# VectorE and ScalarE in program order in two MLPs, with each Strassen bank evicted behind its last product

## The chip, the cores and the metric

The kernel runs on one core of a Trainium2 chip. The metric is the device time of one execution in microseconds; the kernel before took 2025.13 us (median of 3 runs, 2024.51 to 2026.55).

## What is computed

A decoder trunk of two layers over 256 positions of width 2048, all in float32. Each layer is a mixer (a gated MLP in the first, sliding-window attention in the second), a layer norm, an MLP and another layer norm. The change touches the two MLPs:

```python
def sq_relu_mlp(x, w_up, w_down):          # w_up: 2048 x 8192, w_down: 8192 x 2048
    return jnp.square(jax.nn.relu(x @ w_up)) @ w_down

x = layer_norm(DEEPNORM_ALPHA * x + mix, ...)
x = layer_norm(DEEPNORM_ALPHA * x + sq_relu_mlp(x, mlp_w_up[layer], mlp_w_down[layer]), ...)
```

## The kernel before, in words

**Weights.** Every weight arrives as a tile of 128 x 1024 float32 numbers. So that TensorE can multiply at its faster rate without losing float32's accuracy, each is split into two parts: ScalarE casts the high part (`w_hi`, L109) and VectorE subtracts it from the tile to get the low part (`w_lo`, L111). One such pair is an *operand*. The class `Weights` makes operands ahead of their use: there are 9 slots for them in an MLP (5, and 4 lent), and `get()` first fills all slots that are free and then hands out the next operand, so an operand is made when the one nine places before it has been used. Unsplit tiles have 4 buffers of their own, and 4 more in pairs ("wide").

**An MLP** runs in 7 chunks of its inner width. Each of the first six takes 1024 columns:

1. *Up*: 4 products (c = 0 to 3), each of 4 operands, accumulate in a PSUM tile `ps_c`. `act` then adds the two halves of the sum (ScalarE copies one, `part`; VectorE adds, `full`), takes relu and square on ScalarE, splits the result in high and low (`hT`), forms sums and differences of blocks (`sums`) and splits those too.
2. *Strassen round*: half the output columns by Strassen's scheme: 14 operands, here called s0 to s13 in the order in which they are made. Some are sums of tiles, so VectorE adds tiles (L107) before it splits. They make 7 products in 7 PSUM banks, each from two operands: s0 to s6 are the first halves, s7 to s13 the second halves of products o0 to o6. Banks are held in pairs: one PSUM tile holds o0 and o1, the next o2 and o3, then o4 and o5, the last o6 alone.
3. *Evictions*: after the whole round each bank is added to `held` or to `x` on VectorE (L472, L466; in the first chunk four of them are copied by ScalarE instead, L469).
4. *Rows*: the other output columns, two products (n = 2 and 3) of 4 operands each, called r0 to r7 here, in PSUM tiles `ps_r`; each is added to `x` (L421).

PSUM tiles come from two tags with two buffers each, `mm` and `aux`. A round uses all four. The tile of rows n = 2 takes the `mm` buffer of the round's first tile (o0 and o1), so it waits for the evictions of both.

The seventh chunk takes 2048 columns, all by rows. After the sixth, `strassen_end` combines the held products in 8 VectorE operations.

**Order.** The code is written in one sequence, and a scheduler reorders it for each engine by priority and by its own idea of when inputs are ready; each engine then runs its own list strictly in order, with semaphores between the lists. `Weights.dma` keeps the transfers in program order.

Of the kernel before, what the change touches and what calls it, by code (L numbers as in the profile page):

```python
# [11 lines left out]
F32 = mybir.dt.float32  # L12
# [41 lines left out]
class Weights:  # L54
# [4 lines left out]

    def __init__(self, tc, pool, wide, tiles, homes, operands):  # L60
        self.tc, self.nc, self.pool, self.wide = tc, tc.nc, pool, wide
        self.tiles, self.homes, self.operands = tiles, homes, operands
        self.others, self.by_pool = [], ()
        self.borrowed, self.borrowed_from = [], 0
# [29 lines left out]
    def ahead(self, n_split=None):  # L94
# [3 lines left out]
        while self.n_split < min(n_split, len(self.operands)):  # L98
# [53 lines left out]
    def get(self, ahead=None):  # L152
# [3 lines left out]
        self.load(len(self.tiles))  # L156
        hi, lo, kind = self.parts.pop(n)
# [11 lines left out]
def trunk(ctx: ExitStack, tc: tile.TileContext, t, out):  # L169
# [12 lines left out]
    def add_tiles(new):  # L182
        for w in new:
            tiles.append(w)
            homes.append("w")
            operands.append((len(tiles) - 1, None, (len(tiles) - 1,)))

    def add_strassen(new, home):
# [5 lines left out]
        operands.extend([(r, None, ()), (r, r + 1, ()), (r + 1, r + 2, (r + 1,)), (r + 2, None, ()),  # L194
                         (r, r + 2, (r + 2,)), (r + 3, None, ()), (r, r + 3, (r, r + 3))])
# [161 lines left out]
    def gather_halves(ps, bias=None, full=None):  # L357
# [8 lines left out]
        if full is None:  # L366
            full = work.tile([P, 2, S], F32, tag="full", name="full")
# [74 lines left out]
    def strassen_round(hT, groups, n, held, first, scale):  # L442

        tiles = [psum.tile([P, 2, 512], F32, tag=tag, name="ps_s")
# [14 lines left out]
        own = {3: (0, 1, ALU.subtract), 5: (0, 0, ALU.add), 6: (1, 0, ALU.add)}  # L461
        for o, bank in enumerate(banks):
            if o in own:
                tok, c, op = own[o]
                a = x[:, tok, (n + c) * 512:(n + c + 1) * 512]
                nc.vector.scalar_tensor_tensor(out=a, in0=a, scalar=scale, in1=bank,  # L466
                                               op0=ALU.mult, op1=op)
            elif first:
                nc.scalar.copy(out=held[:, HELD.index(o), :], in_=bank)  # L469
            else:  # L470
                a = held[:, HELD.index(o), :]
                nc.vector.tensor_tensor(out=a, in0=bank, in1=a, op=ALU.add)  # L472
# [4 lines left out]
    def strassen_end(n, held):  # L477
# [4 lines left out]
        for out, a, b, op in ((m6, m6, m1, ALU.subtract), (x11, x11, m1, ALU.add),  # L482
# [3 lines left out]
            nc.vector.tensor_tensor(out=out, in0=a, in1=b, op=op)  # L486

    def mlp(x, xT, extra, norm, loads, tags, end):
# [3 lines left out]
        helds = {}  # L492
        for fc, (width, rounds) in enumerate(CHUNKS):
            last = fc == len(CHUNKS) - 1

            def act(c, ps):
                if not rounds:
                    full = gather_halves(ps)
                    nc.vector.scalar_tensor_tensor(out=full, in0=full, scalar=0.0, in1=full,
                                                   op0=ALU.max, op1=ALU.mult)  # L500
                    split(hT[:, 2 * c:2 * c + 2, 0:S], hT[:, 2 * c:2 * c + 2, S:], full)
                    return

                full = gather_halves(ps)
                nc.scalar.activation(out=full, in_=full, func=AF.Relu)
                nc.scalar.activation(out=full, in_=full, func=AF.Square)
                a = full.rearrange("p b (t q) -> p (b t) q", t=NT)
                split(hT[:, c, 0, 0:4], hT[:, c, 1, 0:4], a)
# [445 lines left out]
```

## Time and profile before

| | |
|---|---|
| time, median of 3 runs | 2025.13 us |
| the profiled execution's own time | 2026.41 us |
| its span on the core | 2024.7 us |
| TensorE (PE) busy | 1949.3 us, 96% |
| VectorE (DVE) busy | 1527.6 us, 75% |
| ScalarE (ACT) busy | 1069.5 us, 53% |
| mean granted TensorE clock | 0.981 of full |

PE's busy time counts pipelined products by modelled ends, so it says when PE had work, not how fast it went. The other engines' shares are means over stages that differ; what counts is who is waited for in each stage.

### The profile page before, as it was taken

The numbers are of one execution on the slowest core, as the hardware profiler recorded it, in microseconds if no ns is written. First come the engines' busy times: TensorE is split into PE (matmuls) and PEld (weight loads), VectorE is DVE, ScalarE is ACT, GpSimd is POOL, SyncE is SP. The second block draws the span as 40 slices with busy tenths as digits, with TensorE's granted clock in tenths as the row PEclk, the third lists the DMA queues.
The fourth block names the chain that finished last, engine by engine and source line by source line (L and its number), as shares of the span: only waits on it lengthen the run. The fifth ranks groups of instructions, "written<-read, shape, count | busy, mean of one in ns | idle before, by whom it ended". The sixth has DMA issues, their size and how long they took to land.

```text
span 2024.7 us, 26597 instructions
## 1 busy us (share of the span) xinstructions
PE 1949.3 (96%) x10244; PEld 1670.2 (82%) x10244; DVE 1527.6 (75%) x1749; ACT 1069.5 (53%) x1364; POOL 103.1 (5%) x63
## 2 busy tenths in 40 slices
PE   9999999999999999999998899999999999999997
PEld 7888888878788787888897878888787878878886
DVE  5676689797878869665778997897877868796555
ACT  5445447555555645443456675465555646554431
POOL 0000010000000000000123320100000000000001
PEclk9999999999999999999998899999999999999999
DMA  8755845746556474766443336557565464747662
GB/s 327 271 180 160 286 146 172 255 160 197 176 175 216 156 221 156 240 187 194 149 148 111 97 105 229 177 176 242 175 188 183 157 203 155 252 132 249 187 187 84
DMA packets 105968, 377.57 MB, mean 186 GB/s; under 512 B 12272, under 2 KB 12912, under 8 KB 105840
## 3 DMA queue, kind: packets, MB, share of 16 engines
q1 hardware_dynamic: 105840, 375.86, 56.9%
q8 instruction: 80, 1.31, 0.3%
q14 instruction: 48, 0.39, 0.1%
HBM read 373.72 MB, written 2.10 MB: 186 GB/s over the span
## 4 chain that ended last, share of the span: by engine, by line
issue 82%; PE 8%; DVE 5%; ACT 2%; POOL 1%; DMA 0%; SPq 0%; POOLq 0%; ACTq 0%; DVEq 0%
PE ps_r L274 2%; PE ps_r L272 2%; PE ps_r L273 2%; PE ps_c L309 1%; DVE w_lo L111 1%; ACT p L763 1%; PE ps_c L318 1%; DVE x L400 0%; POOL rstd L381 0%; DVE qT L837 0%; DVE top L754 0%; POOL x L396 0%; DVE es L758 0%; POOL x L395 0%; DMA w_raw<-in_win_v 0%
## 5 line engine op out<-in xcount | busy, mean ns | idle before, releaser
L111 DVE TENSOR_TENSOR w_lo<-w_raw,w_hi 128x1024 fp32r<-128x1024 f32 (+1 forms) x643 | 784.7, 1231 | 340.2 <-ACT w_hi L109 337.6
L109 ACT CAST w_hi<-w_raw 128x1024 fp32r<-128x1024 f32 (+1 forms) x657 | 687.2, 1052 | 581.9 <-PE ps_r L274 208.8
L313 PE MATMUL ps_c<-yT,w_hi 128*128 128x512 f32 x960 | 337.6, 398 | 0.0
L313 PE MATMUL ps_c<-oT,w_hi 128*128 128x512 f32 x960 | 337.6, 398 | 0.0
L272 PE MATMUL ps_r<-w_hi,hT 128*128 128x512 f32 x640 | 255.4, 399 | 31.1 <-DVE held L472 31.1
L318 PE MATMUL ps_c<-oT,w_lo 128*128 128x256 f32 x992 | 272.5, 281 | 0.0
L318 PE MATMUL ps_c<-yT,w_lo 128*128 128x256 f32 x992 | 272.5, 281 | 0.0
L274 PE MATMUL ps_r<-w_hi,hT 128*128 128x512 f32 x640 | 253.5, 396 | 0.0
L273 PE MATMUL ps_r<-w_lo,hT 128*128 128x512 f32 x640 | 253.4, 396 | 0.0
L313 PEld LDWEIGHTS ps_c<-yT,w_hi 128*128 128x128 f32 x960 | 178.9, 188 | 42.1
L313 PEld LDWEIGHTS ps_c<-oT,w_hi 128*128 128x128 f32 x960 | 178.9, 188 | 42.0
L318 PEld LDWEIGHTS ps_c<-yT,w_lo 128*128 128x128 f32 x992 | 187.4, 189 | 2.7
L318 PEld LDWEIGHTS ps_c<-oT,w_lo 128*128 128x128 f32 x992 | 187.4, 189 | 2.7
L272 PEld LDWEIGHTS ps_r<-w_hi,hT 128*128 128x128 f32 x640 | 123.1, 192 | 60.2 <-DVE held L472 18.0
L274 PEld LDWEIGHTS ps_r<-w_hi,hT 128*128 128x128 f32 x640 | 122.9, 192 | 26.3
L273 PEld LDWEIGHTS ps_r<-w_lo,hT 128*128 128x128 f32 x640 | 123.3, 193 | 25.7
L459 PE MATMUL ps_s<-w_hi,hT 128*128 128x512 f32 x336 | 130.9, 389 | 0.0
L458 PE MATMUL ps_s<-w_lo,hT 128*128 128x512 f32 x336 | 130.8, 389 | 0.0
L457 PE MATMUL ps_s<-w_hi,hT 128*128 128x512 f32 x336 | 130.7, 389 | 0.0
L111 DVE TENSOR_TENSOR w_lo<-w_wide,w_hi 128x1024 fp32r<-128x1024 f32 x84 | 101.6, 1222 | 18.0 <-ACT w_hi L109 17.8
L361 ACT COPY part<-ps_c 128x512 f32<-128x512 f32 x72 | 42.3, 588 | 131.5 <-PE ps_c L313 127.3
L109 ACT CAST w_hi<-w_wide 128x1024 fp32r<-128x1024 f32 x84 | 87.3, 1051 | 27.0 <-PE ps_c L313 15.8
(164 smaller groups left out, 2880.4 us busy)
## 6 DMA issues: line engine op xcount, KB each, us to landing
w_raw<-in_up SPq DMA_DIRECT2D x256, 512.0 KB, 4.3
w_raw<-in_down SPq DMA_DIRECT2D x208, 512.0 KB, 3.7
w_wide<-in_down SPq DMA_DIRECT2D x48, 512.0 KB, 6.3
w_raw<-in_win_u SPq DMA_DIRECT2D x32, 512.0 KB, 4.0
w_raw<-in_wout SPq DMA_DIRECT2D x32, 512.0 KB, 4.6
w_raw<-in_wq SPq DMA_DIRECT2D x32, 512.0 KB, 3.7
w_raw<-in_wo SPq DMA_DIRECT2D x32, 512.0 KB, 3.9
w_raw<-in_win_v SPq DMA_DIRECT2D x31, 512.0 KB, 6.6
```

Of the source, the lines that this page charges most:

```text
L109: nc.scalar.copy(out=hi[:, s], in_=raw[:, s])
L111: sub = engine.tensor_tensor(out=lo[:, s], in0=raw[:, s], in1=hi[:, s].bitcast(F32), op=ALU.subtract)
L272: nc.tensor.matmul(out=ps[tok], lhsT=xh, rhs=wh, start=first, stop=False)
L273: nc.tensor.matmul(out=ps[tok], lhsT=xh, rhs=wl, start=False, stop=False)
L274: nc.tensor.matmul(out=ps[tok], lhsT=xl, rhs=wh, start=False, stop=last)
L309: nc.tensor.matmul(out=ps[:, b, 0:S], lhsT=hi[:, w], rhs=stat[:, k, h * S:(h + 1) * S], start=first and h == 0, stop=last and h == 1)
L313: nc.tensor.matmul(out=ps[:, b, :], lhsT=hi[:, w], rhs=stat[:, k, :], start=first, stop=last)
L318: nc.tensor.matmul(out=ps[:, b, 0:S], lhsT=lo[:, w], rhs=stat[:, k, 0:S], start=False, stop=False)
L361: nc.scalar.copy(out=part, in_=ps[:, :, S:])
L457: nc.tensor.matmul(out=banks[o], lhsT=xh, rhs=wh, start=start, stop=False)
L458: nc.tensor.matmul(out=banks[o], lhsT=xh, rhs=wl, start=False, stop=False)
L459: nc.tensor.matmul(out=banks[o], lhsT=xl, rhs=wh, start=False, stop=stop)
```

## The change

In the MLPs (up to the last row product of the seventh chunk) VectorE and ScalarE now keep the order of the code (`manual_schedule`); TensorE and the transfers are scheduled as before. The code is rewritten to suit: a Strassen bank's eviction stands right behind the product that ends it; the sums of weight tiles move ahead by up to one operand, some of them between an operand's cast and its subtraction; and `act` is cut in three: the copy at once, `square` behind the operands that the next `get()` makes, `keep` behind those of the `get()` after it. The 8 operations of `strassen_end` are handed out one at a time behind the up products of the seventh chunk.

```diff
 def ahead(...):
-            at, plus, ended = self.operands[self.n_split]
-            self.load(max(at, plus or 0) + 1)
+            at, before, between, ended = self.operands[self.n_split]
+            self.load(max([at] + [n for pair in before + between for n in pair]) + 1)
...
+            add(before)
             raw = self.raw[at]
-            if plus is not None:
-                nc.vector.tensor_tensor(out=raw, in0=raw, in1=self.raw[plus], op=ALU.add)
             for s in self.pieces(self.n_split):
                 nc.scalar.copy(out=hi[:, s], in_=raw[:, s])
+                add(between)
...
 def get(...):
         self.load(len(self.tiles))
+        for stages in self.later:
+            stages.pop(0)()
+        self.later[:] = [stages for stages in self.later if stages]
...
 def add_strassen(...):
-        operands.extend([(r, None, ()), (r, r + 1, ()), (r + 1, r + 2, (r + 1,)), (r + 2, None, ()),
-                         (r, r + 2, (r + 2,)), (r + 3, None, ()), (r, r + 3, (r, r + 3))])
+        operands.extend([(r, (), (), ()),
+                         (r, ((r, r + 1),), ((r + 1, r + 2),), ()),
+                         (r + 1, (), ((r, r + 2),), (r + 1,)),
+                         (r + 2, (), (), (r + 2,)),
+                         (r, (), (), ()),
+                         (r + 3, (), ((r, r + 3),), (r + 3,)),
+                         (r, (), (), (r,))])
...
 def strassen_round(...):
+        def evict(o, bank):
+            if o in own:
+                tok, c, op = own[o]
+                a = x[:, tok, (n + c) * 512:(n + c + 1) * 512]
+                nc.vector.scalar_tensor_tensor(out=a, in0=a, scalar=scale, in1=bank,
+                                               op0=ALU.mult, op1=op)
+            elif first:
+                nc.scalar.copy(out=held[:, HELD.index(o), :], in_=bank)
+            else:
+                a = held[:, HELD.index(o), :]
+                nc.vector.tensor_tensor(out=a, in0=bank, in1=a, op=ALU.add)
...
                 weights.release()
-        for o, bank in enumerate(banks):
...
+                if g == groups - 1:
+                    evict(o, banks[o])
...
 def mlp(...):
+                part = work.tile([P, 2, S], F32, tag="part", name="part")
+                nc.scalar.copy(out=part, in_=ps[:, :, S:])
+                full = work.tile([P, 2, S], F32, tag="full", name="full")
+                def square():
+                    nc.vector.tensor_tensor(out=full, in0=ps[:, :, 0:S], in1=part, op=ALU.add)
...
+                def keep():
...
+                weights.later.append([square, keep])
...
+            with tc.manual_schedule(engines={mybir.EngineType.DVE, mybir.EngineType.Activation}):
...
                 for c in range(c0, width // 256):
                     act(c, cols_product(xT))
+                    if ends:
+                        ends.pop(0)()
```

What the built program makes of it shows best in the engines' lists around a Strassen round, here the third chunk's of the first MLP; the other rounds differ in details only.

On VectorE, before, from the first add for s8 (`w_wide` is the buffer of the second halves' tiles, `w_raw` that of all others):

```order
L107 TENSOR_TENSOR w_wide<-w_wide 128x1024
L368 TENSOR_TENSOR full<-ps_c,part 128x512
L107 TENSOR_TENSOR w_wide<-w_wide 128x1024
L111 TENSOR_TENSOR w_lo<-w_wide,w_hi 128x1024
L510 TENSOR_TENSOR sums<-full 128x256
L111 TENSOR_TENSOR w_lo<-w_wide,w_hi 128x1024
L246 TENSOR_TENSOR hT<-full,hT 128x512
L512 TENSOR_TENSOR sums<-full,sums 128x128
L111 TENSOR_TENSOR w_lo<-w_wide,w_hi 128x1024
L513 TENSOR_TENSOR sums<-sums,full 128x128
L107 TENSOR_TENSOR w_wide<-w_wide 128x1024
L246 TENSOR_TENSOR hT<-sums,hT 128x512
```

and now, from the same add:

```order
L111 TENSOR_TENSOR w_wide<-w_wide 128x1024 x2
L120 TENSOR_TENSOR w_lo<-w_wide,w_hi 128x1024
L523 TENSOR_TENSOR full<-ps_c,part 128x512
L111 TENSOR_TENSOR w_wide<-w_wide 128x1024
L120 TENSOR_TENSOR w_lo<-w_wide,w_hi 128x1024
L538 TENSOR_TENSOR sums<-full 128x256
L540 TENSOR_TENSOR sums<-full,sums 128x128
L541 TENSOR_TENSOR sums<-sums,full 128x128
L263 TENSOR_TENSOR hT<-full,hT 128x512
L263 TENSOR_TENSOR hT<-sums,hT 128x512
L120 TENSOR_TENSOR w_lo<-w_wide,w_hi 128x1024 x2
```

The steps of `act` for the last up product stood apart, with splits between them; they now stand in two blocks, behind the splits of s8 and of s9.

Further on in the same list, before, up to the third eviction (L472 adds a bank to `held`):

```order
L107 TENSOR_TENSOR w_wide<-w_wide 128x1024
L111 TENSOR_TENSOR w_lo<-w_raw,w_hi 128x1024 x2
L111 TENSOR_TENSOR w_lo<-w_wide,w_hi 128x1024
L111 TENSOR_TENSOR w_lo<-w_raw,w_hi 128x1024 x3
L472 TENSOR_TENSOR held<-ps_s,held 128x512
L111 TENSOR_TENSOR w_lo<-w_raw,w_hi 128x1024
L472 TENSOR_TENSOR held<-ps_s,held 128x512
L111 TENSOR_TENSOR w_lo<-w_raw,w_hi 128x1024
L472 TENSOR_TENSOR held<-ps_s,held 128x512
```

and now (L474 is the same eviction):

```order
L111 TENSOR_TENSOR w_wide<-w_wide 128x1024
L120 TENSOR_TENSOR w_lo<-w_wide,w_hi 128x1024 x2
L120 TENSOR_TENSOR w_lo<-w_raw,w_hi 128x1024 x2
L474 TENSOR_TENSOR held<-ps_s,held 128x512
L120 TENSOR_TENSOR w_lo<-w_raw,w_hi 128x1024
L474 TENSOR_TENSOR held<-ps_s,held 128x512
L120 TENSOR_TENSOR w_lo<-w_raw,w_hi 128x1024
L474 TENSOR_TENSOR held<-ps_s,held 128x512
```

The first eviction stood behind the splits of r0 to r4, the second behind that of r5; now they stand behind those of r1 and of r2.

On TensorE, whose list the scheduler still makes, the first matmul of each piece of work, before, from s7 to the first row product (`ps_s_4362` is the tile of o0 and o1, `ps_s_4363` of o2 and o3, `ps_s_4364` of o4 and o5, `ps_s_4365` of o6; what each waits for is in brackets, where `Activation` is ScalarE):

```order
L457 MATMUL ps_s_4362<-w_hi_4328,hT_3947 128x512
...
L457 MATMUL ps_s_4362<-w_hi_4366,hT_3947 128x512
...
L457 MATMUL ps_s_4363<-w_hi_4377,hT_3947 128x512
...
L457 MATMUL ps_s_4363<-w_hi_4388,hT_3947 128x512
...
L457 MATMUL ps_s_4364<-w_hi_4398,hT_3947 128x512 [waits Activation_49]
...
L457 MATMUL ps_s_4364<-w_hi_4409,hT_3947 128x512 [waits Activation_49]
...
L457 MATMUL ps_s_4365<-w_hi_4419,hT_3947 128x512 [waits Activation_49]
...
L272 MATMUL ps_r_4533<-w_hi_4430,hT_3947 128x512 [waits DVE_49,Activation_49]
```

and now (the four tiles are `ps_s_4359` to `ps_s_4362`):

```order
L487 MATMUL ps_s_4359<-w_hi_4336,hT_3953 128x512
...
L487 MATMUL ps_s_4360<-w_hi_4378,hT_3953 128x512
...
L487 MATMUL ps_s_4361<-w_hi_4407,hT_3953 128x512 [waits Activation_49]
...
L487 MATMUL ps_s_4362<-w_hi_4428,hT_3953 128x512 [waits Activation_49]
...
L487 MATMUL ps_s_4359<-w_hi_4363,hT_3953 128x512 [waits DVE_49]
...
L289 MATMUL ps_r_4541<-w_hi_4438,hT_3953 128x512 [waits DVE_49,Activation_49]
...
L487 MATMUL ps_s_4360<-w_hi_4397,hT_3953 128x512 [waits DVE_49]
...
L289 MATMUL ps_r_4541<-w_hi_4450,hT_3953 128x512 [waits Activation_49]
...
L487 MATMUL ps_s_4361<-w_hi_4417,hT_3953 128x512 [waits DVE_49]
```

The second halves ran as s7, s8, s9 to s13 and then the rows. They now run as s7, s9, s11, s13 (o0, o2, o4, o6: the first of each tile), then s8 (o1) behind a wait on VectorE, then 8 row matmuls behind another, then s10, 14 more row matmuls, s12, and the rest of the rows. In the code the eviction of a tile's first bank now stands ahead of the product into its second bank, and the program keeps that order between the two users of a tile: s8 waits for the eviction of o0, s10 for that of o2, s12 for that of o4. All twelve rounds have this order, with 7 to 10 and 7 to 14 row matmuls at the two places; in the two first chunks the waits for o0, o1, o2 and o4 are on ScalarE's copies.

## Rows read from the trace of the kernel before

**Rows 1.** The page, busy time of each engine over the span

```profile
PE 1949.3 (96%) x10244; PEld 1670.2 (82%) x10244; DVE 1527.6 (75%) x1749; ACT 1069.5 (53%) x1364; POOL 103.1 (5%) x63
```

**Rows 2.** Busy time by stretch: the first MLP and the second

```profile
core 0: us, PE busy (x) PEld busy (x) DVE busy (x) ACT busy (x) POOL busy (x), PEclk, DMA share, GB/s
289.00:1001.00 712.00, 695.48 (x3526) 590.68 (x3525) 541.04 (x606) 381.53 (x437) 3.63 (x4) 0.99 0.59 192
1299.00:2008.00 709.00, 690.07 (x3505) 585.48 (x3505) 531.67 (x599) 372.77 (x427) 1.38 (x2) 0.99 0.58 186
```

**Rows 3.** Waits of PE: who waited for whom, total, times, longest

```profile
PE ps_r L272 <- DVE held L472: 31.1, 9, 4.9
```

**Rows 4.** Timeline of PE, third chunk of the first MLP (start us, us, what)

```profile
499.64 0.40 PE L313 MATMUL ps_c<-yT,w_hi 128*128 128x512 f32 x1
...
505.29 0.40 PE L313 MATMUL ps_c<-yT,w_hi 128*128 128x512 f32 x1
...
508.82 0.39 PE L457 MATMUL ps_s<-w_hi,hT 128*128 128x512 f32 x1
...
510.20 0.39 PE L457 MATMUL ps_s<-w_hi,hT 128*128 128x512 f32 x1
...
527.66 0.39 PE L459 MATMUL ps_s<-w_hi,hT 128*128 128x512 f32 x1
...
531.72 0.47 PE L272 MATMUL ps_r<-w_hi,hT 128*128 128x512 f32 x1 [3.67 <-DVE held L472]
```

**Rows 5.** Busy time and granted clock in stretches behind three such waits

```profile
532.30:535.70 3.40, 3.40 (x10) 2.63 (x9) 3.01 (x4) 2.09 (x2) 0.00 (x0) 0.50 0.80 258
1628.00:1634.80 6.80, 4.43 (x10) 3.47 (x11) 6.01 (x9) 2.55 (x3) 0.00 (x0) 0.50 0.88 292
1445.80:1452.60 6.80, 4.70 (x21) 3.68 (x20) 6.60 (x8) 4.44 (x5) 0.00 (x0) 1.00 0.90 344
```

**Rows 6.** Timeline of VectorE, third chunk, Strassen round

```profile
507.16 1.23 DVE L111 TENSOR_TENSOR w_lo<-w_wide,w_hi 128x1024 fp32r<-128x1024 f32 x1 [1.24 <-ACT w_hi L109]
...
508.42 1.22 DVE L107 TENSOR_TENSOR w_wide<-w_wide 128x1024 f32<-128x1024 f32 x1
...
509.64 0.69 DVE L368 TENSOR_TENSOR full<-ps_c,part 128x512 f32<-128x512 f32 x1
...
512.52 0.42 DVE L510 TENSOR_TENSOR sums<-full 128x256 f32<-128x256 f32 x1
...
518.59 2.36 DVE L111 TENSOR_TENSOR w_lo<-w_wide,w_hi 128x1024 fp32r<-128x1024 f32 x2 [0.57 <-ACT w_hi L109]
...
527.98 1.23 DVE L111 TENSOR_TENSOR w_lo<-w_raw,w_hi 128x1024 fp32r<-128x1024 f32 x1 [0.21 <-ACT w_hi L109]
...
529.12 0.68 DVE L472 TENSOR_TENSOR held<-ps_s,held 128x512 f32<-128x512 f32 x1
...
529.74 1.23 DVE L111 TENSOR_TENSOR w_lo<-w_raw,w_hi 128x1024 fp32r<-128x1024 f32 x1
...
530.88 0.68 DVE L472 TENSOR_TENSOR held<-ps_s,held 128x512 f32<-128x512 f32 x1
```

**Rows 7.** Timeline of ScalarE, the same stretch

```profile
509.02 0.59 ACT L361 COPY part<-ps_c 128x512 f32<-128x512 f32 x1 [1.89 <-PE ps_c L313]
...
509.68 1.06 ACT L109 CAST w_hi<-w_wide 128x1024 fp32r<-128x1024 f32 x1
...
510.64 0.63 ACT L505 ACTIVATE full<-full 128x512 f32<-128x512 f32 x1
...
516.31 0.62 ACT L245 CAST hT<-sums 128x512 fp32r<-128x512 f32 x1 [1.96 <-DVE sums L513]
...
517.50 2.01 ACT L109 CAST w_hi<-w_wide 128x1024 fp32r<-128x1024 f32 x2 [0.57 <-DVE w_wide L107]
```

**Rows 8.** ScalarE's copies of banks in a first chunk (ns min/median/max)

```profile
L469 ACT COPY held<-ps_s x8: 575/588/596, 348.0 to 1359.9; 128x512 f32<-128x512 f32 x8
```

**Rows 9.** The page, weight transfers: KB each, us to landing

```profile
w_raw<-in_down SPq DMA_DIRECT2D x208, 512.0 KB, 3.7
```

More of the change, by code (lines that the diff above doesn't have):

```diff
@@ L496, in act @@
             def act(c, ps):
[L497 to L505, printed above, removed]
@@ L506, in act @@
-                nc.scalar.activation(out=full, in_=full, func=AF.Square)
-                a = full.rearrange("p b (t q) -> p (b t) q", t=NT)
-                split(hT[:, c, 0, 0:4], hT[:, c, 1, 0:4], a)
-                b = work.tile([P, 4, P], F32, tag="part", name="sums")
-                nc.vector.tensor_tensor(out=b[:, 0:2], in0=a[:, 0:4:3],
-                                        in1=a[:, 1:2].to_broadcast([P, 2, P]), op=ALU.subtract)
-                nc.vector.tensor_tensor(out=b[:, 2], in0=a[:, 0], in1=b[:, 1], op=ALU.add)
@@ new lines, in keep @@
+                def keep():
+                    if not rounds:
+                        split(hT[:, 2 * c:2 * c + 2, 0:S], hT[:, 2 * c:2 * c + 2, S:], full)
+                        return
+                    a = full.rearrange("p b (t q) -> p (b t) q", t=NT)
+                    b = work.tile([P, 4, P], F32, tag="part", name="sums")
+                    nc.vector.tensor_tensor(out=b[:, 0:2], in0=a[:, 0:4:3],
+                                            in1=a[:, 1:2].to_broadcast([P, 2, P]), op=ALU.subtract)
+                    nc.vector.tensor_tensor(out=b[:, 2], in0=a[:, 0], in1=b[:, 1], op=ALU.add)
+                    nc.vector.tensor_tensor(out=b[:, 3], in0=b[:, 2], in1=a[:, 2], op=ALU.subtract)
+                    split(hT[:, c, 0, 0:4], hT[:, c, 1, 0:4], a)
+                    split(hT[:, c, 0, 4:8], hT[:, c, 1, 4:8], b)
@@ L541, in mlp @@
-            for n in [n for n in helds if not any(n < 2 * r for _, r in CHUNKS[fc + 1:])]:
-                strassen_end(n, helds.pop(n))
-            for n in range(2 * rounds, 4):
-                st = stats if last else None
-                if n == 3 and last:
-                    last_rows(x, hT, st, scale, partial(norm, stats, hT), end < len(operands))
-                else:
-                    residual(x, rows_product(stat, width // P), n, st, scale)
+            scale = ALPHA if fc == 0 else 1.0
@@ new lines, in mlp @@
+            with tc.manual_schedule(engines={mybir.EngineType.DVE, mybir.EngineType.Activation}):
+                if fc == 0:
+                    for c in range(c0):
+                        act(c, heads[c][0])
+                for c in range(c0, width // 256):
+                    act(c, cols_product(xT))
+                    if ends:
+                        ends.pop(0)()
+                    if c == 2:
+                        weights.in_order = False
+                if last:
+                    borrow(x_tag, end)
+                for n in range(0, 2 * rounds, 2):
+                    first = n not in helds
+                    if first:
+                        helds[n] = extra.tile([P, 4, 512], F32, tag=f"held{n}", name="held")
+                    strassen_round(hT, width // 512, n, helds[n], first, scale)
+                for n in [n for n in helds if not any(n < 2 * r for _, r in CHUNKS[fc + 1:])]:
+                    ends += strassen_end(n, helds.pop(n))
+                for n in range(2 * rounds, 3 if last else 4):
+                    residual(x, rows_product(stat, width // P), n, stats if last else None, scale)
```

51 lines of the change are left out of this document (18 added, 33 removed).

## Prediction, made before the changed kernel ran

> **What bounds the kernel now.** The page first: TensorE is busy 1949.3 of 2024.7 us [rows 1], so only its pauses can be won; VectorE, at 75%, matters where TensorE waits for it. The windows say where: in the two MLPs TensorE is without work for 712.0 - 695.5 = 16.5 us and 709.0 - 690.1 = 18.9 us, with VectorE busy about three quarters of the time [rows 2]. The list of waits names one item for nearly all of it: the first matmul of a row product waits for evictions of `held`, 31.1 us in 9 waits [rows 3]. There are ten rounds whose evictions of `held` are VectorE's, so nine of them wait; the two first chunks, where ScalarE copies (0.59 us each) [rows 8], do not.
>
> The timeline of PE gives one case. An up operand takes TensorE (505.29 - 499.64) / 2 = 2.83 us (the two rows are two operands apart), a Strassen operand 1.38 (508.82 to 510.20; over all fourteen, to 527.66 + 0.23, it is 1.36, and I take 1.365), the last matmul of the round starts at 527.66, and the next starts 4.06 later instead of 0.23 [rows 4]. So a wait costs 0.16 more than its row says (3.83 against 3.67), and nine cost 31.1 + 9 x 0.16 = 32.5 us. VectorE shows why: at 527.98 it is still splitting, and the evictions start at 529.12 and 530.88; the second ends when TensorE goes on [rows 6]. VectorE is behind because a round asks it for 14 splits and 8 adds, 22 x 1.14 = 25 us (1.14 is the step from a split to the next instruction [rows 6]), in 14 x 1.365 = 19.1 us of TensorE's time.
>
> A second cost hangs on the waits: behind the longer ones the granted clock falls to 0.50, the lower level. I count seven such stretches in the MLPs, five of 3.4 us and two of 6.8, and two waits of about 2 us with none behind them [rows 5]. Matmuls take 0.43 instead of 0.23 us there [rows 4, 5]; where TensorE was working that is 1.6 us for a short stretch and 2 for a long one: 5 x 1.6 + 2 x 2 = 12 us.
>
> So at most 32.5 + 12 = 44.5 us are to be had, and the change touches exactly this place.
>
> **The change, part by part.** Matmuls, splits, adds and evictions stay the same in number and size; their order changes. The lists above show two things that pull against each other. On VectorE the second eviction, which opens the `mm` buffer, now has three splits fewer ahead of it: 3 x 1.14 = 3.4 us earlier. On TensorE s8, s10 and s12 now wait for evictions, so s9, s11 and s13 are needed one, two and three places sooner, and the row product that needs the second eviction now stands behind 12 operands instead of 14: 2 x 1.365 = 2.7 us sooner. Which wins is a matter of tenths, so I walk a round of a second to sixth chunk. Time 0 is its first matmul (508.82 in the trace). From engine to engine 0.05 to 0.1 us passes: the first of the two casts from 517.50 ends 1.05 later, at 518.55, and the split that waited for it starts at 518.59 [rows 6, 7]. Steps used: split or add 1.14 to the next, 1.23 to its end; cast 0.96 and 1.05; eviction or `full` 0.61 and 0.69; relu, square, cast of `hT` 0.62 each [rows 6, 7].
>
> *Up to 0.* `act` of the third up product starts when that ends, at -4 x 2.83 = -11.3. In program order it is a chain over both engines: copy -11.1, cast of s4 -10.6, split -9.5, `full` -8.4, relu and square -7.7 to -6.4, cast of s5 to -5.4, split to -4.1, `sums` (0.4 + 0.2 + 0.3) to -3.4, cast of the sums to -2.7, casts of s6 and s7 to -0.8, splits of both -1.7 to 0.6. VectorE starts the first add for s8 at +0.6. Before it was at 508.42, which is -0.4 [rows 6]: 1.0 us lost to the chain.
>
> *From 0 on.* Two adds 0.6 to 2.9 (the cast of s8 falls within), split of s8 3.0, `full` of the last up product 4.1, an add 4.7 to 5.9. Then VectorE waits: the cast of s9 stands behind relu and square (4.9 to 6.2) and ends at 7.1. Split of s9 7.2, `sums` and the two `hT` splits 8.3 to 10.6 (the first needed at 10.7 by s7, the second by s9 at 12.1: both in time), splits of s10 and s11 10.9 to 13.2, the add 13.1 to 14.4, splits of s12, s13, r0, r1 14.3 to 19.0, first eviction 19.0 to 19.6.
>
> *TensorE meanwhile.* s0 to s7 and s9 take it to 9 x 1.365 = 12.3. s11 wants its low part at 12.5 and has it at 13.3; s13 comes at 14.4, its cast (behind the add) ends at 15.5, its low part is there at 16.8; it ends at 18.0. s8 waits for the first eviction, 19.7, and ends at 21.1. VectorE has split r2 by 20.7, but the second eviction reads s8's bank, so it starts at 21.25 and ends at 21.95. The rows start at 22.0. Twelve operands are done that take 12 x 1.365 = 16.4, so the round is **5.6 us** late. Nothing behind it is late once more: the third eviction ends at 23.7, when s10 is due (23.8), the fifth at 27.8 (s12: 27.9), and of the tiles r4 to r7 the first is sent for when r0 is split (17.9) and lands 3.7 us later [rows 9], a cast and a split ahead of its use.
>
> *First chunks.* ScalarE copies the banks behind the casts of r1 and r2 (0.59 each [rows 8]), so no split stands ahead of them: 17.9 for the first, s8 to 19.4, 20.2 for the second: 3.8 late, and about 1 us more because both head products' `act` now run as one block. I take 4.5; from 3.5 to 5.5.
>
> *Nothing elsewhere.* In the seventh chunk VectorE has 1.14 us of split and at most 0.6 of `strassen_end` and `act` work for each 2.83 of TensorE, and TensorE's list of waits has nothing there; the new order stays hidden behind its products, and without that cover would cost at most the 8 x 0.6 us of `strassen_end` in each MLP.
>
> *Half clock.* The new wait is in pieces of 0.8, 1.1, 1.0, 1.7 and 0.9 us with matmuls between them, where single waits of about 2 us were followed by the full clock and those of 2.5 and more by half. Bounds: none of the 12 rounds, or all, 12 x 1.6 = 19 us. The pieces are nearest to the waits of 2 us, so I take a third, 6 us.
>
> *Sum.* 2026.4 - 32.5 - 12 + 10 x 5.6 + 2 x 4.5 + 6 = 2053; that execution was 1.3 above the median, so **2052 us**. The parity point: 44.5 / 12 = 3.7 us late per round with no half clock, the second eviction ending at 20.0 instead of 21.95.
>
> **Rivals.**
> - *VectorE gets there sooner (faster).* One mechanism: ScalarE does not hold up VectorE, so that the wait from 5.9 to 7.2, the 1.0 us before 0 and the 0.6 that the second eviction waits for s8 vanish. The first eviction would start at 16.7, the second end about 19.1, 2.7 us late: 2026.4 - 44.5 + 12 x 2.7 = 2014. For it: before, VectorE idled only 0.57 and 0.21 in this stretch [rows 6]. Against: the lists are strict, and relu, square and a cast stand between `full` and s9. It decides at 20.0. Chance 0.12.
> - *Waits by bank (faster).* The order rows put s8 behind the eviction of o0, which lies in another bank of the same tile. If a bank's eviction held up that bank alone, TensorE would keep s7 to s13 as written and be through them at 14 x 1.365 = 19.1; the second eviction would follow the split of r2 at 20.7 and end at 21.4, each round 2.3 late: 2026.4 - 44.5 + 12 x 2.3 = 2009. The list has the wait, so 0.03. The Trainium skill, PSUM — Partial Sum Buffer, section "PSUM bank collisions raise a hardware error", is the rule behind this rival: it asks for a guard by bank and quadrant, and reports that accesses to different banks ran clean. By that rule the wait of s8 is not needed; no run here shows an access of the kind either way.
> - *The wait goes (faster).* 2026.4 - 44.5 = 1982. It needs the second eviction at 16.4, when VectorE still has r0 to r2 to split. 0.03.
> - *Half clock everywhere (slower still).* If the broken run of 10 us brings the lower level in every round and s8, on which the second eviction hangs, itself runs at it (1.4 more): 2026.4 - 44.5 + 12 x (5.6 + 1.6 + 1.4) = 2085. For it: TensorE works only 4.1 of 9.7 us from 12.3 to 22.0. 0.17.
> - *No change*, 3.7 late: 0.05, since three independent terms would have to give 1.9 us together.
>
> **How the numbers follow.** Forecast 0.60 (its own range 2038 to 2075: 4.7 to 6.2 late in a round, half clock in none to all). A measurement of this kernel tells about 0.2%, 4 us, from no change. Slower 0.60 + 0.17 = 0.77; same 0.05; faster 0.12 + 0.03 + 0.03 = 0.18. The range takes in the waits by bank, the sooner VectorE and the worst case and leaves out the vanished wait: 2008 to 2088.
>
> **What would show it.** Right: PE's waits in the MLPs no longer in one piece ahead of a row product but at s11 and s13 (on the splits), at s8 and the row product (on `held`), about 5 us of idle in each of 12 rounds, some 55 to 65 us in all; VectorE idle over 1 us ahead of the split of s9. Wrong: a second eviction that ends before 20 us into the round, or TensorE going through s11 and s13 without a pause; then the walk is too slow, and the result is at or under 2025.

## The result and the profile after

The changed kernel takes 2083.56 us (median of 4 runs, 2081.99 to 2085.94) where the kernel before takes 2024.91 us beside it (4 runs, 2024.51 to 2026.55): 1.0289 times as long, 95% interval 1.0271 to 1.0307. The forecast was 2052 us, the loss 58.6 us in place of 27. Its span is 2080.6 us, the mean granted clock 0.973. Two disturbed executions, 8079.87 us of the early eviction alone and 2727.64 us of the four stages, are left out of the times below.

The page of the changed kernel, busy time, answers to [rows 1]:

```profile
PE 1979.4 (95%) x10244; PEld 1671.7 (80%) x10244; DVE 1538.3 (74%) x1749; ACT 1061.2 (51%) x1364; POOL 103.0 (5%) x63
```

The windows of its two MLPs answer to [rows 2], with the same columns:

```profile
289.00:1029.00 740.00, 709.85 (x3522) 591.38 (x3521) 546.05 (x606) 377.80 (x437) 3.04 (x3) 0.97 0.57 185
1327.00:2064.00 737.00, 709.16 (x3500) 589.91 (x3501) 534.62 (x596) 368.13 (x426) 1.51 (x2) 0.97 0.55 179
```

Each MLP is 28 us longer; the window of the attention between them is 298 us in both kernels. TensorE has the same matmuls and is *busy* 14 and 19 us longer, and without work 30 and 28 us in place of 16.5 and 18.9. By the sums at the end of this section, 17.8 of those 33 us are matmuls at the lower clock. Most of the rest comes with the new breaks: ahead of a break a matmul counts with its whole 0.39 us, though in an unbroken stream the next one starts after 0.23. The list of waits of PE answers to [rows 3]; the one item of before is gone, and four stand in its place:

```profile
PE ps_s L488 <- DVE w_lo L120: 20.2, 24, 1.0
PE ps_s L487 <- ACT w_hi L117: 12.0, 13, 1.0
PE ps_s L487 <- DVE held L474: 11.4, 10, 1.4
...
PE ps_r L289 <- DVE held L474: 8.7, 10, 0.9
```

The timeline of PE, third chunk of the first MLP (round from 520.23), shows the five pieces one by one, the answer to [rows 4]:

```profile
532.49 0.43 PE L487 MATMUL ps_s<-w_hi,hT 128*128 128x512 f32 x1
533.87 0.50 PE L488 MATMUL ps_s<-w_lo,hT 128*128 128x512 f32 x1 [0.94 <-DVE w_lo L120]
...
534.89 0.39 PE L489 MATMUL ps_s<-w_hi,hT 128*128 128x512 f32 x1
536.26 0.50 PE L487 MATMUL ps_s<-w_hi,hT 128*128 128x512 f32 x1 [0.98 <-ACT w_hi L117]
537.52 0.50 PE L488 MATMUL ps_s<-w_lo,hT 128*128 128x512 f32 x1 [0.76 <-DVE w_lo L120]
...
538.55 0.39 PE L489 MATMUL ps_s<-w_hi,hT 128*128 128x512 f32 x1
540.39 0.50 PE L487 MATMUL ps_s<-w_hi,hT 128*128 128x512 f32 x1 [1.44 <-DVE held L474]
...
541.65 0.39 PE L489 MATMUL ps_s<-w_hi,hT 128*128 128x512 f32 x1
542.91 0.47 PE L289 MATMUL ps_r<-w_hi,hT 128*128 128x512 f32 x1 [0.88 <-DVE held L474]
```

From start to start, less the 0.23 us of a matmul, the pauses are 1.15 (s11), 1.14 and 1.03 (s13), 1.61 (s8) and 1.03 (row product); the first matmul behind a pause takes 0.1 more. That makes 6.4 us. The timeline of VectorE there answers to [rows 6]:

```profile
527.59 1.22 DVE L120 TENSOR_TENSOR w_lo<-w_wide,w_hi 128x1024 fp32r<-128x1024 f32 x1 [1.17 <-ACT w_hi L117]
...
531.45 2.36 DVE L120 TENSOR_TENSOR w_lo<-w_wide,w_hi 128x1024 fp32r<-128x1024 f32 x2 [0.26 <-ACT w_hi L117]
533.85 1.22 DVE L111 TENSOR_TENSOR w_wide<-w_wide 128x1024 f32<-128x1024 f32 x1
...
537.38 2.35 DVE L120 TENSOR_TENSOR w_lo<-w_raw,w_hi 128x1024 fp32r<-128x1024 f32 x2
539.65 0.68 DVE L474 TENSOR_TENSOR held<-ps_s,held 128x512 f32<-128x512 f32 x1
...
542.08 0.69 DVE L474 TENSOR_TENSOR held<-ps_s,held 128x512 f32<-128x512 f32 x1 [0.61 <-PE ps_s L489]
```

The splits of r0 and r1 (`w_raw`, 537.38) stand ahead of the first eviction, which starts 19.42 us into the round. The second, which waits for s8, starts at 21.85 here. This round is the exception in one thing: its clock stays full. In the other nine rounds whose evictions are VectorE's, s8 runs at half clock and the second eviction starts at 23.1; the fifth round (from 706.66):

```profile
729.78 0.69 DVE L474 TENSOR_TENSOR held<-ps_s,held 128x512 f32<-128x512 f32 x1 [1.89 <-PE ps_s L489]
```

Behind the pauses the clock falls; two such stretches, in windows, answer to [rows 5]:

```profile
725.10:735.30 10.20, 7.97 (x19) 5.56 (x18) 6.35 (x7) 2.37 (x3) 0.00 (x0) 0.50 0.67 214
445.20:452.00 6.80, 5.92 (x14) 4.19 (x15) 4.52 (x5) 2.09 (x2) 0.00 (x0) 0.50 0.72 242
```

Ten of the twelve rounds have one: six of 10.2 us, two of 6.8, two of 3.4, where before there were five of 3.4 and two of 6.8. The third round and the seventh have none, though the third has the same five pieces as the fifth. A stretch of 10.2 holds up to 19 matmuls that take 0.43 in place of 0.23 us: 3.8 us.

For the rest two sums are used, each over the 45 us from the start of each of the 12 rounds: *pauses*, the steps between matmuls beyond their length, and *half clock*, by how much matmuls in stretches at 0.50 take longer. Before they are 32.8 and 12.4 us, after 73.4 and 30.2. The difference, 58.4 us, is the loss as far as these sums can tell (58.6 between the medians, 55.9 between the two profiled executions).

### The profile page after: what moved, and what is told of

Its sections match the earlier page's. It is cut to its first block, busy times and chain, and to the rows that moved or that the text cites. A ratio compares the mean times of both kernels' runs of the same rounds, so it can differ in the third digit from the quotient of the medians.

```text
span 2080.6 us, 26679 instructions
## 1 busy us (share of the span) xinstructions
PE 1979.4 (95%) x10244; PEld 1671.7 (80%) x10244; DVE 1538.3 (74%) x1749; ACT 1061.2 (51%) x1364; POOL 103.0 (5%) x63
## 4 chain that ended last, share of the span: by engine, by line
issue 80%; PE 10%; DVE 6%; ACT 2%; POOL 1%; DMA 0%; SPq 0%; POOLq 0%; ACTq 0%; DVEq 0%
PE ps_r L289 2%; PE ps_r L291 2%; PE ps_r L290 2%; DVE w_lo L120 1%; PE ps_c L326 1%; ACT p L795 1%; PE ps_c L335 1%; DVE qT L869 0%; DVE pT L263 0%; DVE top L786 0%; POOL x L412 0%; POOL rstd L397 0%; POOL x L411 0%; DVE o L834 0%; DVE swap L716 0%
## 5 line engine op out<-in xcount | busy, mean ns | idle before, releaser
L117 ACT CAST w_hi<-w_raw 128x1024 fp32r<-128x1024 f32 (+1 forms) x657 | 679.8, 1048 | 541.8 <-PE ps_r L291 145.1
L487 PE MATMUL ps_s<-w_hi,hT 128*128 128x512 f32 x336 | 142.2, 423 | 23.3 <-ACT w_hi L117 12.0
L488 PE MATMUL ps_s<-w_lo,hT 128*128 128x512 f32 x336 | 140.7, 419 | 20.2 <-DVE w_lo L120 20.2
L489 PE MATMUL ps_s<-w_hi,hT 128*128 128x512 f32 x336 | 138.8, 413 | 1.3 <-DVE hT L263 1.3
L120 DVE TENSOR_TENSOR w_lo<-w_wide,w_hi 128x1024 fp32r<-128x1024 f32 x84 | 101.6, 1221 | 17.6 <-ACT w_hi L117 17.2
L487 PEld LDWEIGHTS ps_s<-w_hi,hT 128*128 128x128 f32 x336 | 67.1, 200 | 52.2 <-ACT w_hi L117 19.8
```

Source lines behind the costliest of these rows:

```text
L487: nc.tensor.matmul(out=banks[o], lhsT=xh, rhs=wh, start=start, stop=False)
L488: nc.tensor.matmul(out=banks[o], lhsT=xh, rhs=wl, start=False, stop=False)
L489: nc.tensor.matmul(out=banks[o], lhsT=xl, rhs=wh, start=False, stop=stop)
```

## The experiments

**The theories.** Theory A was the first: the evictions' new place makes o1, o3 and o5 wait, TensorE takes s11 and s13 early, the broken pauses bring the half clock. Rival B: the program order makes splits and evictions late, in whatever order TensorE goes. Later expectations cut B finer. C says that program order is the loss, D that the staged activations or the new sums are. Within C, the cause may be evictions behind splits in VectorE's queue (C1, C3), or the two queues waiting for each other in turn (C2). All runs with an interval are in one table (us; *added* are matmuls of no use; the sums of the early eviction alone are from its second run). Each ratio is to runs of the kernel before beside it, whose medians lie between 2023.8 and 2026.1, so differences between rows hold to some 2 us:

| kernel | time | ratio to before, 95% | pauses | half clock | added |
|---|---|---|---|---|---|
| evictions behind the round, rest as changed | 2143.74 | 1.0564 to 1.0599 | 138.6 | 20.5 | |
| early eviction alone | 2010.85 | 0.9912 to 0.9945 | 25.5 | 1.6 | |
| changed, no program order | 2009.75 | 0.9905 to 0.9942 | 24.7 | 3.2 | |
| order on VectorE only | 2032.77 | 1.0024 to 1.0074 | 44.6 | 8.1 | |
| order on ScalarE only | 2023.70 | 0.9987 to 1.0006 | 37.0 | 5.2 | |
| order on both, no stages | 2089.11 | 1.0299 to 1.0340 | 82.9 | 24.7 | |
| order on both, four stages | 2045.95 | 1.0080 to 1.0125 | 52.8 | 12.4 | |
| four stages, no rows ahead | 2039.70 | 1.0066 to 1.0096 | 58.1 | 3.2 | |
| far partners | 2071.29 | 1.0215 to 1.0246 | 61.9 | 27.0 | |
| far partners, no rows ahead | 2053.29 | 1.0123 to 1.0153 | 49.6 | 24.7 | |
| far partners, early eviction alone | 2017.28 | 0.9942 to 0.9972 | 30.5 | 11.0 | |
| far partners, no program order | 2013.02 | 0.9920 to 0.9955 | 26.0 | 8.0 | |
| filled at s11, s13 and s8 | 2061.95 | 1.0165 to 1.0199 | 21.9 | 0 | 57.3 |
| filled at s8 | 2076.70 | 1.0242 to 1.0292 | 56.6 | 18.1 | 19.1 |
| filled at s11 and s13 | 2062.56 | 1.0172 to 1.0202 | 39.9 | 0 | 38.2 |

### The place of the evictions

Evictions back behind the round, the rest of the change kept:

```diff
-                if g == groups - 1:
-                    evict(o, banks[o])
+        for o, bank in enumerate(banks):
+            evict(o, bank)
```

> The changed kernel with the seven evictions back behind the round; program order on VectorE and ScalarE, the operands' new sums and the staged activations stay. The order of the products in the program is then the written one. Theory A (the place of the evictions makes o1, o3 and o5 wait, TensorE takes s11 and s13 before VectorE has split them, and the broken pauses bring the half clock): the pauses inside the rounds go, the old wait of the row product (about 3.6 us in 9 rounds) stays, and the time is that of before within 1.5%, 1995 to 2040 us. Theory B (program order makes the splits late whatever the order of the products): waits of 1 us and more for w_lo stay in the last group of each round, and the time is 2055 us or more.

The early eviction alone, on the kernel before (the same lines the other way round, with `evict` taken over):

> The kernel before with one part of the change: each bank is evicted behind its last product; VectorE and ScalarE stay with the scheduler, sums and activations as before. The program has the products of the last group in the order o0, o2, o4, o1, o3, o6, o5. Theory A: the place of the evictions by itself makes most of the loss: pauses in three or four pieces of each round and half clock in them, 2045 to 2085 us. Theory B: without program order VectorE evicts and splits in time, no pieces, and the time is 1980 to 2030 us.

Both go against theory A. Without the early evictions the changed kernel is not better but 60 us worse, and the early eviction alone makes the kernel before faster by 15 us (2026.07 beside it), though the program then takes the last group in the order o0, o2, o4, o1, o3, o6, o5. For rival B both times are as it said, but not its sign: the first run has no wait for `w_lo` in a round's last group. Its waits of PE say where its time goes:

```profile
PE ps_r L289 <- DVE held L474: 114.3, 10, 11.8
```

In program order all seven evictions stand behind the splits for every slot that the round has freed, so the row product waits 11.4 us where it waited 3.5 before [rows 3]. The early eviction alone was run once more, for its trace:

> The kernel before with the early evictions alone, once more for a usable trace: the time is 2011 us within 5; evictions of o0 begin 13 to 15 us after the round's start, the row product no longer waits 3.6 us, and what is left are pauses of 1.0 to 2.5 us in the last group, 20 to 30 us in 12 rounds.

One run, 2004.98 us. Its first eviction of the third chunk starts 14.3 us into the round, pauses add up to 25.5 us, and the row product's wait (in the list of waits of PE) is:

```profile
PE ps_r L272 <- DVE held L458: 8.5, 6, 2.7
```

### Program order on both engines, on one, on none

The edit is one argument; for none the `with` line goes:

```diff
-            with tc.manual_schedule(engines={mybir.EngineType.DVE, mybir.EngineType.Activation}):
+            with tc.manual_schedule(engines={mybir.EngineType.DVE}):
```

> The whole changed kernel without its program order: the scheduler sets the order on VectorE and ScalarE in the MLPs again; early evictions, new sums and staged activations stay. Theory C (program order is the loss): the time is near that of the early eviction alone, 1995 to 2025 us. Theory D (the staged activations or the new place of the sums among the operands are the loss): 2050 us or more. Theory A (the place of the evictions): also 2050 us or more, which the run of the early eviction alone already speaks against.

> The changed kernel with program order on VectorE alone; ScalarE is the scheduler's. Theory C1 (the loss is the place of splits and evictions in VectorE's queue): the loss stays, 2065 to 2090 us. Theory C2 (the loss comes from the two queues waiting for each other in turn, ScalarE 1.8 us at each sum and 1.8 us at each activation for VectorE and VectorE 1.2 us for the cast behind it): with one of them free, half of it or more goes, 2010 to 2050 us.

> The changed kernel with program order on ScalarE alone; VectorE is the scheduler's. Theory C1: nearly all of the loss goes, 2005 to 2025 us. Theory C2: about half goes, 2025 to 2060 us. If ScalarE's own order is the loss, 2065 us or more, and then program order on VectorE alone costs little.

Without program order the changed kernel takes 2009.75 us, like the early eviction alone. Theory C holds and D falls: the staged activations and the new places of the sums neither cost nor give anything that shows there. Program order costs 73.8 us. VectorE's alone costs 23.0, ScalarE's alone 14.0, together 37; so half of the loss, 36.8 us, comes only when both are in order (33.8 by the ratios). C1 fell on the first, and the second is within its range. C2 came out right for VectorE; for ScalarE more of the loss went (60 us) than the half it gave, and the time is 1.3 us under its range. Of the 36.8 the sums give 16.5 to pauses (48.7 more than without order, against 19.9 and 12.3) and 20.1 to half clock (27.0 against 4.9 and 2.0).

The timeline of VectorE without program order, third chunk, round from 508.3:

```profile
520.79 1.22 DVE L120 TENSOR_TENSOR w_lo<-w_raw,w_hi 128x1024 fp32r<-128x1024 f32 x1
521.92 0.69 DVE L474 TENSOR_TENSOR held<-ps_s,held 128x512 f32<-128x512 f32 x1
522.52 1.22 DVE L120 TENSOR_TENSOR w_lo<-w_raw,w_hi 128x1024 fp32r<-128x1024 f32 x1
523.65 1.22 DVE L120 TENSOR_TENSOR w_lo<-w_wide,w_hi 128x1024 fp32r<-128x1024 f32 x1
```

The first eviction starts 13.6 us into the round, 5.8 sooner than in the changed kernel, ahead of the split of a second-half operand (`w_wide`, 523.65) and of all row operands but one. With VectorE alone in order it starts at 17.1, with ScalarE alone at 13.6.

### The two queues waiting for each other

In program order ScalarE's list of waits has two items that the kernel before has not, or not at this size (ScalarE waits for the sum of the halves, and for the sums of blocks):

```profile
ACT full L525 <- DVE full L523: 85.6, 46, 2.6
ACT hT L262 <- DVE sums L541: 83.5, 48, 1.8
```

Each stage of an activation crosses between the engines inside one `get()`; the casts of the next operands stand behind it, and VectorE waits for those (the 1.17 us above). Two runs on that:

```diff
-                weights.later.append([square, keep])
+                square()
+                keep()
```

> The changed kernel with each activation in one piece behind its product, as in the kernel before, in program order. If the three stages between operands give back part of what program order costs: slower than the changed kernel, 2095 us or more (each of the 48 activations then holds both queues for the chain of about 6 us between them). If the stages are worth nothing in program order as without it (2009.8 and 2011.0 us): 2075 to 2090 us.

and four stages, so cut that the engine that goes first in a stage does not need the other's work of the same stage, but for the last subtraction (`add_halves`: the sum on VectorE; `square`: Relu and Square; `sums`: first cast and the three sums; `low`: second cast and the two subtractions):

```diff
-                weights.later.append([square, keep])
+                weights.later.append([add_halves, square, sums, low] if rounds else [whole, keep])
```

> The changed kernel, program order on both engines, with each activation in four stages in place of three: the sum of the halves, Relu and Square, the three sums with the first cast, the second cast with the two subtractions. No stage then waits for the other engine in the middle, but for the last subtraction. Theory C2 (a large part of the loss is that the two queues wait for each other in turn around the activations, so that VectorE comes late to s9 to s13): a third or more of the 74 us between both and no program order goes, 2030 to 2060 us. Rival C3 (the waits in turn are slack, and the loss is only the evictions behind the splits): 2070 to 2090 us.

An activation in one piece costs 5.5 us against three stages, within the range that stood for no worth, and the two intervals overlap; four stages give 37.6 us against three. Both items are gone from the head of ScalarE's list, the first eviction starts at 17.5, pauses fall by 20.6 us and half clock by 17.8. So the way the activations are cut is shown to be about half of what program order costs. That the waits in turn are the reason fits both lists; but four stages also put the last steps of an activation one `get()` later, and no run keeps the two apart. In the last run the row operands are kept out of the way as well (`get(6 - o)` in the last group, as below):

> The four stages, and in a round's last group the operands split ahead only up to s13, so that no row operand's split stands ahead of an eviction. If the two causes add, it is 15 to 35 us faster than the four stages alone, and may reach 2000 to 2040 us; if the row product then waits for its own operands instead, the two are within 8 us.

It gained 6.3 us, less than half of the least that adding up would give. Half clock falls to 3.2 us, but pauses rise by 5.3, since the row product now waits for its own operands (waits of PE, for ScalarE's casts, behind which the splits come):

```profile
PE ps_r L289 <- ACT w_hi L117: 11.1, 8, 1.4
```

Some 30 us of what program order costs are left in this kernel (2039.70 against 2009.75); no run here takes them away.

### The two-bank tiles

Other partners in the tiles, so that no bank shares one with the bank evicted just ahead of it:

```diff
-        banks = [tiles[o // 2][:, o % 2, :] for o in range(7)]
+        banks = [tiles[(0, 1, 2, 3, 0, 1, 2)[o]][:, o // 4, :] for o in range(7)]
```

> The changed kernel with other partners in the two-bank PSUM tiles: o0 with o4, o1 with o5, o2 with o6, o3 alone, in place of o0 with o1 and so on. Evictions stay behind the last product. No product then waits for the eviction just ahead of it, and the program has the products in the written order. Theory A: neither the pauses in pieces (73 us) nor most of the old wait of the row product (33 us) nor their half clock (30 us) are left: 1980 to 2000 us, with up to 15 us more if the two last evictions hold up the row product. Theory B (the splits of s11 and s13 are late because of program order alone): the waits for w_lo stay, 2040 us or more.

TensorE now goes in the written order and still stands, in one piece, behind the first eviction (waits of PE):

```profile
PE ps_s L487 <- DVE held L474: 50.1, 10, 5.0
```

Theory A loses here for good: TensorE's order and the tile mates together are worth 12 us of the 59. Theory B has the time right and its sign wrong: the waits for `w_lo` are gone, the wait for the eviction has come in their place. The eviction starts 19.4 us into the round as in the changed kernel, because VectorE's queue has not changed. To move it, the last group looks ahead less far:

```diff
-                hi, lo = weights.get()
+                hi, lo = weights.get(6 - o if g == groups - 1 else None)
```

> The kernel with the far partners (changed kernel, o0 with o4 and so on), and in a round's last group the operands are split ahead only up to s13, so that the row operands r0, r1 and later ones stand behind the evictions in VectorE's program order, not ahead of them. Theory C (program order puts the eviction of o0 behind the splits of all operands for which a slot was free, here s12, s13, r0 and r1, and the product that waits for it is late by their length): r0 and r1 are 2.35 us in the trace, so the wait of 5.0 us ahead of o4 falls to about 2.6 us, 28 us in 12 rounds, and the time to 2030 to 2055 us; the row product may then wait up to 1 us for its own operands. Rival (the eviction is late because of its own length or of PSUM, not of the queue ahead of it): the 5.0 us stay, and the time is 2065 to 2080 us.

The same item in its list of waits of PE:

```profile
PE ps_s L487 <- DVE held L474: 38.8, 10, 3.9
```

The time is as expected, 18 us less, the wait only 1.1 us shorter in place of 2.35: the split of r0 was issued by the `get()` of s6 and is still ahead (the timeline has one `w_raw` split there, 1.22 us). With the scheduler in charge the partners matter little:

> The kernel before with early evictions and far partners alone (no program order, no staged activations, sums as before). The program then has the products in the written order, and no bank waits for the eviction just ahead of it. If what is left of the loss in the early eviction alone (2011 us) is the wait of o1, o3 and o5 for their tiles: 1980 to 2003 us, no row product waiting 3.6 us. Rival (o4 to o6 wait as long for o0 to o2, or VectorE's evictions among the splits make those late): 2005 to 2025 us.

> The changed kernel without program order and with far partners. If staged activations and new sums are worth something by themselves, it is faster than the early eviction and far partners on the kernel before by 3 to 15 us: 1975 to 1995 us; if they are worth nothing, the two are within 3 us of each other.

The first missed: o4, o5 and o6 wait for evictions instead (22.5 us in 11 waits), and far partners are some 6 us slower than near ones, at the edge of what the intervals tell apart. The second is neither of its two cases: 4.3 us faster than the first, but 18 us above the range given, and the intervals of the two runs overlap.

### The half clock

Matmuls of no use in the pauses, into the bank that the round leaves empty:

```diff
+FILL = {4: 5, 6: 9, 7: 7}
...
+        def fill(n):
+            for _ in range(n):
+                nc.tensor.matmul(out=tiles[3][:, 1, :], lhsT=hT[:, 0, 0, 0, :], rhs=hT[:, 0, 0, 0:4, :],
+                                 start=True, stop=True)
...
                 hi, lo = weights.get()
+                fill(FILL.get(o, 0) if g == groups - 1 else 0)
...
                 if g == groups - 1:
+                    if o == 6:
+                        fill(FILL[7])
                     evict(o, banks[o])
```

The 7 behind o6 are those ahead of s8. The two other runs have `FILL = {7: 7}` and `{4: 5, 6: 9, 7: 0}`.

> The changed kernel with matmuls of no use in the four pauses of each round: 5 ahead of the product with s11, 9 ahead of that with s13, 7 ahead of that with s8 (128x512 each, into the bank that the round leaves unused, at 0.2275 us 4.8 us per round, where the pauses are 4.3 to 4.9 us). The order of all other products is that of the changed kernel. Theory A (the clock falls because of the pauses): no stretch at half clock inside the rounds, the 73 us of waits are nearly all replaced by the added matmuls, and the time falls by the 30 us of half clock to 2050 to 2065 us, though TensorE has 57 us more to do. Rival (the clock falls for another reason, such as the load of the other engines or the rate of the products around the pauses): the half-clock stretches stay and the time is 2083 us or more.

> The changed kernel with 7 matmuls of no use ahead of the product with s8 only; the pauses ahead of s11 and of s13 stay. The half-clock rows of the changed kernel cost 30 us. If one piece more or less decides how long the clock stays down: 5 to 20 us of it are left, 2062 to 2078 us. If the pause at s8, the longest, brings it by itself: none is left, 2052 to 2062 us. If the pauses at s11 and s13 bring it: it stays, 2078 to 2088 us.

> The changed kernel with 5 and 9 matmuls of no use ahead of the products with s11 and s13 only; the pauses at s8 and at the row product stay. If the number of pieces decides: little half clock is left, 0 to 10 us, 2053 to 2066 us. If the pause at s8 brings it by itself: 20 to 30 us stay, 2075 to 2088 us.

Windows of 45 us from a round's start, the columns as above (PEclk third from the end). The third and the fifth round of the changed kernel:

```profile
520.20:565.20 45.00, 40.00 (x171) 31.37 (x170) 38.60 (x41) 24.11 (x27) 0.00 (x0) 1.00 0.51 163
706.70:751.70 45.00, 40.12 (x155) 30.87 (x154) 35.90 (x39) 22.28 (x25) 0.00 (x0) 0.89 0.45 143
```

The fifth round with all three places filled:

```profile
702.60:747.60 45.00, 44.12 (x192) 35.30 (x191) 38.66 (x41) 24.10 (x27) 0.00 (x0) 1.00 0.52 162
```

The fifth round with s11 and s13 filled:

```profile
702.40:747.40 45.00, 42.68 (x185) 34.00 (x184) 38.63 (x41) 24.11 (x27) 0.00 (x0) 1.00 0.50 163
```

The fourth round with s8 alone filled, one of those that still fall:

```profile
611.80:656.80 45.00, 41.73 (x167) 32.83 (x166) 36.81 (x40) 23.64 (x26) 0.00 (x0) 0.92 0.46 150
```

252 added matmuls (57.3 us at 0.2275) make the kernel 21.6 us *faster*: no stretch at half clock is left in the rounds. With s8 filled alone seven of the twelve rounds still have one, none over 6.8 us. With s11 and s13 filled none has, though the 1.6 us at s8, the longest pause, is still there. So the fall goes with the three pieces at s11 and s13, and the one at s8 behind them makes it longer and more frequent. Program order on VectorE alone lies between: in ten rounds it has one piece of 1.03 us at s13, 1.6 at s8 and about 1.0 at the row product, and five of these fall, four for 3.4 us and one for 6.8, while the last two pieces alone (s11 and s13 filled) brought none in ten. Its second round and its third:

```profile
419.00:464.00 45.00, 41.92 (x181) 33.35 (x180) 38.51 (x41) 25.09 (x27) 0.00 (x0) 1.00 0.54 174
509.30:554.30 45.00, 41.91 (x176) 33.31 (x176) 37.37 (x41) 25.43 (x27) 0.00 (x0) 0.96 0.51 165
```

That the pauses cause it is shown; why the same pieces bring it in one round and not in another is open.

## Why the prediction was off by as much again

**The walk of a round: right where the clock stays full.** VectorE idle over 1 us ahead of the split of s9: 1.17. First eviction at 19.0 into the round: 19.42. The second ending at 21.95: 22.54 in the third chunk, but 23.8 in the nine rounds where s8 runs at half clock. Pieces of 0.8, 1.1, 1.0, 1.7 and 0.9 at s11, s13, s8 and the row product: 1.15, 1.14, 1.03, 1.61, 1.03. The old 44.5 us went (45.2 by the sums here).

**The size of the waits: a little low.** 10 x 5.6 + 2 x 4.5 = 65 against 73.4 us. The largest part is what the walk left out, the 0.1 us that the first matmul behind a pause takes longer, four or five times in each of twelve rounds: 5 to 6 us.

**The half clock: the step that failed.** "The pieces are nearest to the waits of 2 us, so I take a third, 6 us." Measured are 30.2, above the bound of 19 as well. Two things were wrong in it. It priced a stretch by those of before (1.6 us), which follow a single pause; behind the pieces six stretches are 10.2 us long and cost up to 3.8 each. And it compared the pieces one by one with single waits. The runs with filled pauses show otherwise: the three pieces at s11 and s13, none over 1.15 us in the ten rounds with evictions by VectorE, still bring the fall in five of these ten when s8 is filled; the 1.6 us at s8, the piece nearest to a wait of 2 us, brings none without them. With 73.4 and 30.2 for 65 and 6 the forecast's sum is 2084.

**The rival that came nearest.** "Half clock everywhere" said that s8, on which the second eviction hangs, would run at the lower level; it did, in nine of the ten rounds with evictions by VectorE, and the lower level came in ten of twelve rounds. Its 2085 is in part luck: it adds 67 us for the waits and 36 for half clock, where 73.4 and 30.2 were measured.

**What was right for a reason not seen in full.** The prediction told the wait as a contest of a sooner eviction against a sooner need by TensorE, with the chain over both engines worth 1.0 us ahead of the round and 1.3 in it. The runs turn the weights round: the earlier eviction is a gain of 15 us by itself and of 60 under program order, TensorE's new order with its tile mates costs about 12 us under program order and nothing that shows without it, and program order loses 74, half of it only where both engines keep it. The rival "VectorE gets there sooner", 2014 us, is close to what the change gives without its program order, 2010.

**Other rivals.** Far partners take away the mates that "waits by bank" was about: 2071, not 2009, since the eviction is late for whoever waits for it; a wait by bank itself was not tried. Elsewhere nothing changed that shows, as forecast: the two sums over the rounds give the loss to within 2.5 us.

## What to carry to other kernels

Program order on one engine of a pair that hands work back and forth cost about 1% here, on both nearly 4%, twice the two together; before fixing an order, cut each stage so that it needs only what the other engine did a stage ago, and count what a look-ahead puts ahead of an eviction. A moved eviction and a fixed order are two changes: tried apart, the one was worth -0.7% and the other +3.7%. And short pauses are not to be priced one by one: those that follow each other closely have to be counted together, and even filling them with useless matmuls was faster here than leaving them.

## What the runs showed of the hardware

Single pauses do not tell the clock. Without program order a pause of 2.3 us (second round, 17.6 us in) was followed by the full clock, and one of 2.1 us (sixth round) by 3.4 us at half. Several short ones can bring it too. With s8 filled, the pieces at s11 and s13 (three of 1.0 to 1.15 us within some 5 us in ten rounds, four of 0.8 to 1.2 in the two first chunks) were followed by 3.4 to 6.8 us at half in seven rounds of twelve. With more behind them, in the changed kernel, it was up to 10.2 us, and in two rounds none. The Trainium skill, TensorE: Matmul & The Clock Gate, section "A second HAM failure mode: psum-queue depth-cycling", tells of a kernel whose clock went up and down because TensorE was idle briefly and often between groups of matmuls; the traces here agree, and the runs with filled pauses show the cause by taking it away.
